# Expert outputs added from 128 stacked rows, and the overfull path as one loop on the chip

## The chip, the cores and the metric

The kernel runs on one NeuronCore of a Trainium2 chip. The metric is the device time of one execution in microseconds (us). One core has the engines TensorE (PE, with its weight loads shown as PEld), VectorE (DVE), ScalarE (ACT), GpSimd (POOL), and SyncE (SP), whose queue issues most DMAs.

## The reference, cut to what matters

Two transformer-like blocks run one after the other on 256 tokens of 1024 features, in fp32. What the change touches is the mixture of experts that closes each block: block 1 has 16 experts, block 2 has 32, and every token goes to two of them.

```python
# block 1
hid = silu(einsum('td,edf->tef', t, w_gate)) * einsum('td,edf->tef', t, w_up)
hid = hid * gates[:, :, None]
y = einsum('tef,efd->td', hid, w_down)     # 256 tokens, 16 experts, 1024 -> 512 -> 1024
# block 2, for each of 32 experts
hdn = silu(xt @ wg) * (xt @ wu)
acc = acc + cw[:, None] * (hdn @ wd)
```

## The kernel before, in words

**Weights.** All weights come in over the SP queue (`Stream`, L128) in pieces of 1 MiB, in a fixed order, into a pool of 21 tiles of 128x2048 fp32. An expert has six pieces: two each of gate, up and down.

**Dispatch.** An expert holds at most `cap` tokens, 64 in block 1 and 32 in block 2. The router gives each token a slot number in each of its experts. `dispatch` (L1140) gathers the tokens of four experts of block 1 (eight of block 2) into columns, with 0/1 matrices `pm` that DVE makes by comparing slots with an iota (L1125); the result is normalized on the way out of PSUM by DVE (L1147) and ACT (L1149).

**One expert** (`experts`). `gate_up` (L1215) multiplies by the gate and up weights into one PSUM bank; `hidden` copies (L1156), transposes (L1161; in block 2 L1163), and makes silu(gate) x up (L1166, L1168). `slots_T` makes `PT`, the 0/1 matrix from slots to tokens, (L1179, L1181, L1185), and each slot's gate value `gc` (L1183, L1187). `back()` then multiplies by the down weights (`down`, L1224). The result `py` stands on 128 rows: the slots with output features 0 to 511 (half q = 0) on rows 0 to 63, the same slots with features 512 to 1023 (q = 1) on rows 64 to 127.

**Adding an expert's output.** `gated` multiplies `py` by gate value and gain (L1197, DVE), rounds it to fp32r, the high part `yh` (L1198, ACT), and subtracts to have the low part `yl` (L1199, DVE), so that two fp32r products carry the fp32 value. `add` multiplies by `PT` into the accumulators `acc`: in block 1 `to_features` (L1242), 16 matmuls of 64 rows and 256 columns for an expert, namely two halves x four feature blocks x high and low; in block 2 `to_rows` (L1253), 8 matmuls of 64 rows and 512 columns. Both operands have 64 rows, one half at a time. In the program, an expert's addition stands between the two halves of the next expert's `gate_up`; the last expert goes by halves of its output (L1301).

**Overfull experts.** Ahead of `experts`, `overflow` handles what is over `cap`. A flag, true if any expert has more than `cap` tokens, is loaded into a register of every engine (L1313), and all five engines take `tc.If` (L1314). Its body loops over the experts on the chip (L1315); within, Python unrolls one copy of the code for each further 64 tokens: three copies in block 1, four in block 2. With these inputs the flag is 0 in both blocks, so the body is jumped over.

**Order.** A scheduler of the language decides where each engine's instructions stand, from their dependences and its own costs, so an edit in one function can move instructions of others.

## Time and profile before

| | before |
|---|---|
| median of 3 runs | 1361.27 us (1361.03 to 1363.59) |
| the profiled execution's own time | 1368.25 us |
| its span in the trace | 1366.7 us |
| mean granted TensorE clock | 0.934 |
| PE, DVE, ACT, POOL busy | 87%, 41%, 23%, 7% of the span |
| moved by DMA | 404.15 MB, 296 GB/s over the span |

The profile is of one execution; its span is from the first to the last instruction. "PEclk" is the TensorE clock that was granted, as a share of full speed. A wait of an engine is given with its releaser, as [3.79 <-PEq L1314]: 3.79 us idle, ended by PE's sequencer at line 1314. A `q` behind an engine's name is its sequencer, which takes branches and issues DMAs. A matmul's shape is written as weights, then output: 64\*128 64x256 has 64 rows of input, 128 columns of weights, and 256 columns that stream. An fp32 matmul of 128\*64 shows as two records.

### The profile page before, as it was taken

The numbers are of one execution on the slowest core, as the hardware profiler recorded it, in microseconds if no ns is written. First come the engines' busy times: TensorE is split into PE (matmuls) and PEld (weight loads), VectorE is DVE, ScalarE is ACT, GpSimd is POOL, SyncE is SP. The second block draws the span as 40 slices with busy tenths as digits, with TensorE's granted clock in tenths as the row PEclk, the third lists the DMA queues.
The fourth block names the chain that finished last, engine by engine and source line by source line (L and its number), as shares of the span: only waits on it lengthen the run. The fifth ranks groups of instructions, "written<-read, shape, count | busy, mean of one in ns | idle before, by whom it ended". The sixth has DMA issues, their size and how long they took to land. (4 is left out here: it accounts for less than half of the span.)

```text
span 1366.7 us, 20989 instructions
## 1 busy us (share of the span) xinstructions
PE 1194.2 (87%) x8690; PEld 731.7 (54%) x8690; DVE 556.7 (41%) x1418; ACT 314.4 (23%) x629; POOL 101.2 (7%) x111
## 2 busy tenths in 40 slices
PE   5899967899999986988999999879888887788786
PEld 2777757444444434886778888844323332233222
DVE  4487653322214127688655747442211221121112
ACT  3345331111101014552332224221101110010001
POOL 2421110000001003001510010000000000000000
PEclk7999888899999995999999999989997999999987
DMA  8777657799984952451236528759999999999995
GB/s 297 288 286 277 249 204 276 301 419 419 420 320 173 421 239 96 152 182 34 71 133 216 183 88 335 289 218 419 419 419 419 420 419 419 421 419 418 420 419 211
DMA packets 60520, 404.15 MB, mean 296 GB/s; under 512 B 7329, under 2 KB 7585, under 8 KB 14465
## 3 DMA queue, kind: packets, MB, share of 16 engines
q1 hardware_dynamic: 58464, 400.58, 73.5%
q10 hardware_dynamic: 1824, 2.00, 0.5%
q8 instruction: 72, 1.18, 0.3%
q0 software_dynamic: 128, 0.13, 0.1%
q14 instruction: 32, 0.25, 0.1%
HBM read 401.64 MB, written 1.05 MB: 295 GB/s over the span
## 5 line engine op out<-in xcount | busy, mean ns | idle before, releaser
L1215 PE MATMUL a<-u,u 128*32 128x512 f32 (+1 forms) x1536 | 311.4, 619 | 14.5 <-DMA u<-in_expert_w_up 7.5
L1197 DVE SCALAR_TENSOR_TENSOR gs<-a,gc,gt 128x512 f32<-128x512 f32 (+1 forms) x50 | 37.5, 750 | 304.6 <-PE a L1224 293.1
L1224 PE MATMUL a<-u,hid 128*32 128x512 f32 (+1 forms) x736 | 127.8, 619 | 37.6 <-DMA u<-in_expert_w_down 37.6
L1215 PEld LDWEIGHTS a<-u,u 128*32 128x32 f32 (+1 forms) x1536 | 71.2, 120 | 150.3 <-issue 119.7
L684 PE MATMUL a<-u,u 128*128 128x256 f32 x656 | 144.2, 298 | 2.2 <-DVE u L629 2.2
L684 PE MATMUL a<-u,hi 128*128 128x256 f32 x640 | 137.4, 306 | 0.4 <-ACT u L1529 0.4
L684 PEld LDWEIGHTS a<-u,u 128*128 128x128 f32 x656 | 107.3, 199 | 12.7 <-issue 9.2
L1156 ACT COPY gs<-a 128x512 f32<-128x512 f32 x48 | 28.1, 585 | 355.3 <-PE a L1215 353.1
L684 PEld LDWEIGHTS a<-u,hi 128*128 128x128 f32 x640 | 100.0, 193 | 15.6 <-issue 8.9
L1224 PEld LDWEIGHTS a<-u,hid 128*32 128x32 f32 (+1 forms) x736 | 31.1, 118 | 116.0 <-issue 47.8
L1198 ACT CAST u<-gs 128x512 fp32r<-128x512 f32 (+1 forms) x50 | 30.9, 618 | 186.1 <-DVE gs L1197 186.1
L1253 PE MATMUL acc<-u,PT 64*128 64x512 f32 x256 | 60.8, 468 | 13.0 <-ACT u L1198 11.2
L629 DVE TENSOR_TENSOR u<-u,hi 128x1024 fp32r<-128x1024 f32 x48 | 61.6, 1291 | 15.2 <-ACT hi L628 14.7
L628 ACT CAST hi<-u 128x1024 fp32r<-128x1024 f32 x48 | 49.8, 1047 | 68.9 <-PE a L684 60.6
L1185 DVE CAST PT<-a 128x256 fp32r<-128x256 f32 x48 | 20.4, 424 | 108.3 <-PE acc L1253 63.0
L1253 PEld LDWEIGHTS acc<-u,PT 64*128 64x128 f32 x256 | 31.8, 206 | 53.4 <-DVE u L1199 16.6
L1179 DVE TENSOR_SCALAR gp<-iota,rslot 128x128 f32<-128x128 f32 x96 | 23.0, 283 | 86.8 <-PE a L1183 78.1
L908 PE MATMUL a<-u,u 128*128 128x256 f32 x256 | 50.3, 318 | 9.2 <-DVE u L629 8.0
L629 POOL TENSOR_TENSOR u<-u,u 128x512 fp32r<-128x512 f32 (+1 forms) x22 | 44.0, 2018 | 129.8 <-ACT u L628 129.8
L1163 PEld LDWEIGHTS a<-sel,gs 128*128 128x128 f32 x256 | 35.1, 212 | 28.6 <-issue 27.1
L908 PEld LDWEIGHTS a<-u,u 128*128 128x128 f32 x256 | 41.5, 222 | 10.3 <-DVE u L629 8.2
L1181 PEld LDWEIGHTS a<-ident,gp 128*128 128x128 f32 x96 | 11.4, 141 | 65.0 <-issue 31.5
(447 smaller groups left out, 1691.2 us busy)
## 6 DMA issues: line engine op xcount, KB each, us to landing
u<-in_expert_w_gate SPq DMA_DIRECT2D x96, 1024.0 KB, 19.9
u<-in_expert_w_up SPq DMA_DIRECT2D x96, 1024.0 KB, 19.9
u<-in_expert_w_down SPq DMA_DIRECT2D x96, 1024.0 KB, 19.9
u<-in_ada_w SPq DMA_DIRECT2D x32, 1024.0 KB, 7.0
u<-in_w_in SPq DMA_DIRECT2D x19, 1024.0 KB, 4.9
u<-in_ada_w SPq DMA_DIRECT2D x32, 512.0 KB, 4.3
u<-in_attn_w_in SPq DMA_DIRECT2D x12, 512.0 KB, 8.9
u<-in_attn_w_in SPq DMA_DIRECT2D x6, 1024.0 KB, 7.0
```

Source lines behind the costliest of these rows:

```text
L628: nc.scalar.copy(h[:, o], w[:, o])
L629: (nc.vector if e == "v" else nc.gpsimd).tensor_tensor(l[:, o], w[:, o], h[:, o].bitcast(F32), ALU.subtract)
L684: c.nc.tensor.matmul(ps, a[:, k, c0:c0 + n], b[:, k], start=k == 0 and i == 0, stop=k == kn - 1 and i == 2)
L908: self.c.nc.tensor.matmul(ps[:, j * S:(j + 1) * S], a[:, k, j * P:(j + 1) * P], b[:, k], start=k + j + i == 0, stop=k == KD - 1 and i == 2 ...
L1156: nc.scalar.copy(gs, pg)
L1163: nc.tensor.matmul(pt[:, f * w:(f + 1) * w], gs[:, f * P:(f + 1) * P], fl(c.sel), start=True, stop=True)
L1179: nc.vector.tensor_scalar(gp[:, t], it, slot[:, t], None, ALU.is_equal)
L1197: nc.vector.scalar_tensor_tensor(out=y[o], in0=py[o], scalar=gc[o], in1=gt[o], op0=ALU.mult, op1=ALU.mult)
L1198: nc.scalar.copy(yh[o], y[o])
L1215: c.nc.tensor.matmul(pg[r:r + cap], xe[:, k0 + k, x0:x0 + cap], w[:, k, :], start=k0 + k < nk, stop=k0 + k >= KD - nk)
L1224: c.nc.tensor.matmul(py[r:r + cap], hT[:, f], w[:, f - f0, q * 512:(q + 1) * 512], start=f < nk, stop=f >= 4 - nk)
L1253: c.nc.tensor.matmul(acc[:, 2 * t + q], PT[H2[q], t * P:(t + 1) * P], y[H2[q], :], start=False, stop=stop and i == 1, skip_group_check=True)
```

## The change

Three things change.

1. **Stacked rows.** The high part of half q stays on that half's 64 rows and goes to column block q of a tile, and the low part is written to the other 64 rows of the same column block. One matmul of 128 rows then adds high and low together, against `PT`, which holds the same slots in both halves of its rows. `to_features` issues 8 matmuls instead of 16 for an expert, `to_rows` 4 instead of 8. `gated` casts and subtracts twice 64x512 in place of once 128x512, and the subtraction reads rows of one half and writes rows of the other.
2. **A loop on the chip.** The body of `overflow` stands once, in a second loop on the chip that lowers the slot by 64 each time, in place of three or four unrolled copies.
3. **Which side comes first.** `tc.If` gets `preferred_fallthrough_block=False`: behind the compare comes the false, empty side, an unconditional branch over the body.

Counted in the two built programs, PE's jump over the body goes from 677 to 262 instructions in block 1 and from 827 to 254 in block 2; DVE's first jump before is over 86. PE has 17577 instructions in all, 19069 before.

```diff
@@ -1188,23 +1188,26 @@
     return PT, gc
 
 
-def gated(c, ep, py, gc, gt, o=slice(0, P)):
-
-    nc = c.nc
-    yh, yl = c.ys[0]
+def gated(c, ep, py, gc, gt, qs=(0, 1)):
+
+
+    yy = c.ys[0]
     c.ys.reverse()
     y = ep.tile([P, 512], F32, name="gs", bufs=2)
-    nc.vector.scalar_tensor_tensor(out=y[o], in0=py[o], scalar=gc[o], in1=gt[o], op0=ALU.mult, op1=ALU.mult)
-    nc.scalar.copy(yh[o], y[o])
-    nc.vector.tensor_tensor(yl[o], y[o], yh[o].bitcast(F32), ALU.subtract)
-    return yh, yl
+    o = slice(0, P) if len(qs) == 2 else H2[qs[0]]
+    c.nc.vector.scalar_tensor_tensor(out=y[o], in0=py[o], scalar=gc[o], in1=gt[o], op0=ALU.mult, op1=ALU.mult)
+    for q in qs:
+        c.nc.scalar.copy(yy[H2[q], q], y[H2[q]])
+    for q in qs:
+        c.nc.vector.tensor_tensor(yy[H2[1 - q], q], y[H2[q]], yy[H2[q], q].bitcast(F32), ALU.subtract)
+    return yy
 
 
 def split_rows(c):
 
     c.uys = c.un.raw()
-    y = c.uys.bitcast(F32R).rearrange("p (i a d) -> p i a d", i=2, a=2)
-    c.ys = [(y[:, i, 0], y[:, i, 1]) for i in range(2)]
+    y = c.uys.bitcast(F32R).rearrange("p (i q d) -> p i q d", i=2, q=2)
+    c.ys = [y[:, i] for i in range(2)]
 
 
 def gate_up(c, pg, xe, x0, cap, w, a, k0, kn):
@@ -1234,24 +1237,22 @@
 
 def to_features(c, acc):
 
-    def add(ys, PT, stop=False, qs=(0, 1)):
+    def add(yy, PT, stop=False, qs=(0, 1)):
         for q in qs:
             for b in range(4):
                 fb = 4 * q + b
-                for i, y in enumerate(ys):
-                    c.nc.tensor.matmul(acc[:, fb // 2, (fb % 2) * S:(fb % 2 + 1) * S], y[H2[q], b * P:(b + 1) * P],
-                                       PT[H2[q], :], start=False, stop=stop and i == 1, skip_group_check=True)
+                c.nc.tensor.matmul(acc[:, fb // 2, (fb % 2) * S:(fb % 2 + 1) * S], yy[:, q, b * P:(b + 1) * P], PT,
+                                   start=False, stop=stop, skip_group_check=True)
     return add
 
 
 def to_rows(c, acc):
 
-    def add(ys, PT, stop=False, qs=(0, 1)):
+    def add(yy, PT, stop=False, qs=(0, 1)):
         for q in qs:
             for t in range(2):
-                for i, y in enumerate(ys):
-                    c.nc.tensor.matmul(acc[:, 2 * t + q], PT[H2[q], t * P:(t + 1) * P], y[H2[q], :],
-                                       start=False, stop=stop and i == 1, skip_group_check=True)
+                c.nc.tensor.matmul(acc[:, 2 * t + q], PT[:, t * P:(t + 1) * P], yy[:, q],
+                                   start=False, stop=stop, skip_group_check=True)
     return add
 
 
@@ -1299,7 +1300,7 @@
         for f in range(4):
             o = (q * nk + f % nk) * cap
             nc.tensor.matmul(py[o:o + cap], hT[:, f], w[:, f], start=f < nk, stop=f >= 4 - nk)
-        add(gated(c, ep, py, gc, gt, H2[q]), PT, True, (q,))
+        add(gated(c, ep, py, gc, gt, (q,)), PT, True, (q,))
         end(q)
 
 
@@ -1311,13 +1312,14 @@
     wg, wu, wd = (c.I[f"expert_w_{a}{x}"][:NE * 2 * P * 2048].rearrange("(e h p n) -> e h p n", h=2, p=P, n=2048)
                   for a in ("gate", "up", "down"))
     rv = nc.values_load(flag[0:1, 0:1], min_val=0, max_val=1)
-    with tc.If(rv > 0):
+    with tc.If(rv > 0, preferred_fallthrough_block=False):
         with tc.For_i(0, NE, 1) as e:
-            for base in range(cap, S, 64):
-                so = ep.tile([P, 2, 1], F32, name="oso")
-                go = ep.tile([P, 2, 1], F32, name="ogo")
-                nc.vector.tensor_scalar(so, slot[:, :, bass.ds(e, 1)], -float(base), None, ALU.add)
-                nc.vector.tensor_copy(go, gate[:, :, bass.ds(e, 1)])
+            so = ep.tile([P, 2, 1], F32, name="oso")
+            go = ep.tile([P, 2, 1], F32, name="ogo")
+            nc.vector.tensor_scalar(so, slot[:, :, bass.ds(e, 1)], 64.0 - cap, None, ALU.add)
+            nc.vector.tensor_copy(go, gate[:, :, bass.ds(e, 1)])
+            with tc.For_i(0, -(-(S - cap) // 64), 1):
+                nc.vector.tensor_scalar(so, so, -64.0, None, ALU.add)
                 xo = ep.tile([P, KD, 64], F32, name="oxe")
                 dispatch(c, ep, tok, so, 0, 1, 64, xo)
                 PT, gc = slots_T(c, ep, so, go, 64)
```

In what follows, lines of the changed kernel are two or three further on: gate_up is L1218, down L1227, the addition of block 1 L1244, the flag's load L1314 and the branch L1315.

**Where the order moves.** PE's queue around the first overflow path, before, from the last dispatch matmuls to the loop's head (`acc<-u,ident` puts the residual into the accumulator):

```order
L1140 MATMUL a<-pm,u_662 128x256 x16
L1450 MATMUL acc<-u_67,ident 128x512 x4
L1313 TENSOR_LOAD rfl_2207
L1314 COMPARE_AND_BRANCH
L1315 COMPARE_AND_BRANCH
L1315 UNCONDITIONAL_BRANCH x2
L2408 BRANCH_PREFETCH_HINT
```

and now:

```order
L1140 MATMUL a<-pm,u_662 128x256 x16
L1452 MATMUL acc<-u_67,ident 128x512 x4
L1314 TENSOR_LOAD rfl_2207
L1315 COMPARE_AND_BRANCH
L1315 UNCONDITIONAL_BRANCH
L1316 COMPARE_AND_BRANCH
L1316 UNCONDITIONAL_BRANCH x2
L2410 BRANCH_PREFETCH_HINT
```

Behind the compare (L1315) there is now an unconditional branch, and then the two nested loops' heads (L1316 and, further on, L1321); before, the outer loop's head followed the compare.

PE's queue in block 1's experts, an addition near the end of the down matmuls, before:

```order
L1224 MATMUL a<-u_2615,hid 64x512 x4
L1224 MATMUL a<-u_2137,hid 64x512 x4
L1161 MATMUL a<-ident,gs 128x128 x4
L1215 MATMUL a<-u_2138,u_2143 64x512
L1242 MATMUL acc<-PT,u_2213 128x256 x16
L1215 MATMUL a<-u_2139,u_2143 64x512
```

and now:

```order
L1227 MATMUL a<-u_2374,hid 64x512 x4
L1227 MATMUL a<-u_2137,hid 64x512 x4
L1161 MATMUL a<-ident,gs 128x128 x4
L1181 MATMUL a<-ident,gp 128x128 x2
L1218 MATMUL a<-u_2138,u_2143 64x512
L1244 MATMUL acc<-PT,u_2213 128x256 x4
L1183 MATMUL a<-rgate_2195,gp 128x1 x2
L1244 MATMUL acc<-PT,u_2213 128x256 x4
L1218 MATMUL a<-u_2139,u_2143 64x512
```

The addition is 4 + 4 matmuls in place of 16, and the next expert's slot matrices (L1181, L1183) have come ahead of it and between its halves; before, they stood further on, between the halves of gate_up.

PE's queue in block 1's experts, the last dispatch of four experts (L1140), before its first part:

```order
L1215 MATMUL a<-u_2214,u_2143 64x512
L1140 MATMUL a<-pm,u_661 128x256 x4
L1140 MATMUL a<-pm,u_662 128x256
L1215 MATMUL a<-u_2215,u_2143 64x512
L1140 MATMUL a<-pm,u_662 128x256 x3
L1215 MATMUL a<-u_2615,u_2143 64x512
L1215 MATMUL a<-u_2215,u_2143 64x512
```

and now all of it:

```order
L1227 MATMUL a<-u_2137,hid 64x512 x4
L1227 MATMUL a<-u_2138,hid 64x512 x4
L1161 MATMUL a<-ident,gs 128x128 x4
L1140 MATMUL a<-pm,u_661 128x256 x12
L1140 MATMUL a<-pm,u_662 128x256 x6
L1140 MATMUL a<-pm,u_661 128x256 x4
L1140 MATMUL a<-pm,u_662 128x256 x10
L1218 MATMUL a<-u_2139,u_2143 64x512
```

Before, eight of the 32 matmuls stood 5 + 3 in the middle of a gate_up and the other 24 after the next L1161; now all 32 stand in one run behind L1161.

## Rows read from the trace of the kernel before

**Rows 1.** Windows by stage: us, busy of PE PEld DVE ACT POOL, PEclk, DMA, GB/s.
```profile
256.00:262.00 6.00, 5.95 (x20) 2.29 (x22) 1.99 (x8) 0.00 (x0) 0.00 (x0) 0.72 1.02 422
300.00:400.00 100.00, 98.62 (x534) 46.38 (x532) 21.68 (x58) 13.65 (x27) 0.00 (x0) 1.00 1.01 414
...
963.00:1345.00 382.00, 313.33 (x1881) 119.75 (x1871) 71.72 (x185) 41.66 (x88) 0.00 (x0) 0.95 1.01 419
1314.80:1328.50 13.70, 12.47 (x42) 4.47 (x43) 2.22 (x5) 0.89 (x2) 0.00 (x0) 0.50 1.01 420
```

**Rows 2.** The timeline of PE, 275 to 505: first row after each end of fourteen periods.
```profile
277.88 0.44 PE L1181 MATMUL a<-ident,gp 128*128 128x128 f32 x2
...
500.23 0.66 PE L1161 MATMUL a<-ident,gs 128*128 128x128 f32 x4
```

**Rows 3.** The branch on the flag (L1314), by engine: ns min/median/max, first and last start.
```profile
L1314 PEldq COMPARE_BRANCH  x2: 3359/5289/7219, 248.4 to 900.7; - x2
L1314 DVEq COMPARE_BRANCH  x2: 56/64/72, 249.8 to 901.8; - x2
```

**Rows 4.** The timeline around the first branch: start, us, instruction, [idle before <- releaser].
```profile
248.67 3.59 PE L1450 MATMUL acc<-u,ident 128*128 128x512 f32 x8
...
256.05 6.21 PE L1215 MATMUL a<-u,u 128*64 128x512 f32 x20 [3.79 <-PEq L1314]
```

**Rows 5.** The timeline around the second branch.
```profile
899.97 1.22 PE L1140 MATMUL a<-pm,u 128*128 128x256 f32 x8 [0.81 <-DVE rcm L1097]
...
901.81 0.56 ACT L1149 ACTIVATE u<-a,mod,A2b 128x256 f32<-128x256 f32 x1 [1.46 <-DVE u L1147]
...
904.45 5.34 PE L1215 MATMUL a<-u,u 128*32 128x512 f32 x32 [3.26 <-PEq L1314]
```

**Rows 6.** The timeline of PE, one dispatch and one addition between two halves of gate_up.
```profile
305.97 4.05 PE L1140 MATMUL a<-pm,u 128*128 128x256 f32 x32
...
313.54 1.79 PE L1242 MATMUL acc<-PT,u 64*128 64x256 f32 x16
315.26 3.65 PE L1215 MATMUL a<-u,u 128*64 128x512 f32 x16
```

**Rows 7.** The timeline of an addition that follows close on its down matmuls.
```profile
402.38 0.75 DVE L1197 SCALAR_TENSOR_TENSOR gs<-a,gc,gt 128x512 f32<-128x512 f32 x1 [6.55 <-PE a L1224]
...
403.17 0.62 ACT L1198 CAST u<-gs 128x512 fp32r<-128x512 f32 x1 [3.61 <-DVE gs L1197]
...
403.82 0.69 DVE L1199 TENSOR_TENSOR u<-gs,u 128x512 fp32r<-128x512 f32 x1 [0.68 <-ACT u L1198]
403.85 0.38 PE L1242 MATMUL acc<-PT,u 64*128 64x256 f32 x1
...
404.56 1.66 PE L1242 MATMUL acc<-PT,u 64*128 64x256 f32 x15 [0.33 <-DVE u L1199]
```

**Rows 8.** The timeline of PE, a dispatch split around a pair of gate_up.
```profile
358.66 0.86 PE L1140 MATMUL a<-pm,u 128*128 128x256 f32 x5
359.44 1.07 PE L1215 MATMUL a<-u,u 128*64 128x512 f32 x2
...
361.00 3.65 PE L1215 MATMUL a<-u,u 128*64 128x512 f32 x14
```

**Rows 9.** The timeline of PE, the fifth period, and of the last expert's second half.
```profile
349.08 0.30 PE L1181 MATMUL a<-ident,gp 128*128 128x128 f32 x1 [0.67 <-DVE gc L1187]
...
511.71 2.37 PE L1242 MATMUL acc<-PT,u 64*128 64x256 f32 x15 [1.86 <-DVE u L1199]
```

**Rows 10.** The timeline of the tail.
```profile
1356.88 1.41 DVE L1199 TENSOR_TENSOR u<-gs,u 64x512 fp32r<-64x512 f32 x2
1356.93 0.61 ACT L1198 CAST u<-gs 64x512 fp32r<-64x512 f32 x1 [0.23 <-DVE gs L1197]
...
1357.62 0.96 PE L1253 MATMUL acc<-u,PT 64*128 64x512 f32 x3 [0.36 <-DVE u L1199]
...
1359.98 2.07 PE L1253 MATMUL acc<-u,PT 64*128 64x512 f32 x4 [1.40 <-ACT u L2228]
```

## The prediction

> **What bounds the kernel now.** I read the windows by stage first, then the branch line of the overflow path, then the engine timelines around it, around an addition in each block, and at the end. Block 1's experts (some 256 to 505 us) are bound by PE: 98.6 us busy of 100 at clock 1.00 [rows 1]. The fourteen expert periods from 277.88 to 500.23 take 222.35 us [rows 2]. Block 2's experts are bound by the weight DMA: 419 GB/s at a DMA share of 1.01 over 382 us, with PE busy 313.3 of them at clock 0.95 [rows 1]. PE work that is saved there is worth nothing; an earlier start of the DMA stream and a shorter tail are. Between the stages, up to the second branch, both kernels have the same order on PE, so time gained in block 1 is carried through.
>
> The sum is made against the profiled execution, whose own time is 1368.25 us (span 1366.7); the median of the runs is 1361.27, 7 us below it. The sum of differences is applied to both.
>
> **The branch around the overflow path, block 1.** The flag is 0, so no engine runs the body. DVE's compare-and-branch took 56 to 72 ns, PE's took 7219 and 3359 ns [rows 3]; counted in the built programs, DVE jumps over 86 instructions there, PE over 677 in block 1 and 827 in block 2. DVE is at its branch at 249.8 [rows 3]; PE's last matmuls before its own start at 248.67 and end by 252.26, and yet its next one comes at 256.05, after 3.79 us in which it waited for its own sequencer [rows 4]. So what is late is PE's jump. After, the body stands once instead of three and four times and the additions in it are halved: PE jumps over 262 and 254 instructions, and the flag's false side comes right behind the compare. No row shows a jump of 262. It lies between DVE's (0.06 us) and PE's (3.4 us). I take DVE's and leave 0.4 us of meeting of the engines: **-3.4 us**. [...]
>
> After the idle time the granted clock is 0.72 over 256 to 262 [rows 1]: twenty matmuls of gate_up take 6.21 us [rows 4], where sixteen at full clock take 3.65, so twenty 4.56 [rows 6]. Without the gap the clock has no reason to fall, since PE was at 1.00 before it: **-1.65 us**.
>
> **Each addition in block 1.** Sixteen 64-row matmuls take 1.72 us from start to start (313.54 to 315.26), 0.108 each. 128-row matmuls of the same 256 columns take 4.05 us for 32 [rows 6], some 0.125 each. Eight stacked ones are at least 8 x 0.108 = 0.86, at most 1.72. I take 8 x 0.125 plus 0.14 for the change of tile shape = 1.14, by the nearest row: -0.58 each, over fourteen periods **-8.1 us**.
>
> [...]
>
> What pays for it: ACT casts twice 64x512 (0.61 us each) in place of 128x512 once (0.62 [rows 7]), DVE subtracts twice 64x512 (1.41 us for two [rows 10]) in place of once (0.69 [rows 7]). Both have room (DVE 21.7, ACT 13.7 us busy of 100 [rows 1]). The subtraction now writes to the other 64 partitions. No row shows such an operation; between 0.70 (the same shape, straight) and 1.4 (twice it), I take 0.70, the nearest shape. In the first five periods half a gate_up, 3.5 us, lies between the end of down and the addition, which covers the chain of 3.0 us (multiply 0.75, two casts, two subtractions).
>
> **The order in block 1.** Fewer matmuls make the scheduler place things otherwise.
> - Two dispatches of four experts (L1140) are split before: eight of 32 matmuls stand 5 + 3 around one pair of gate_up, 2.34 us from 358.66 to 361.00 [rows 8]. That pair alone takes 1.00 instead of 0.44, the eight need 1.00 in one run, and the fourteen that follow lose another 0.5. In the new order all 32 stand together: 2.34 - 1.00 - 0.44 + 0.5 = 1.4 each, **-2.8**.
> - The fifth period holds two selections (L1181, L1183) back to back, with 0.67 us of idle time between them [rows 9], the down matmuls split around them; after, they stand apart: **-1.0**.
> - In six periods the addition follows close on the down matmuls: one pair of gate_up, then the first matmul at 403.85 and the other fifteen at 404.56, because DVE's subtraction is not done [rows 7]: 0.71 - 0.11 = 0.60 lost. After, the order is L1161, L1181, a pair of gate_up, four matmuls, L1183, four matmuls. PE gets to the first four some 0.6 + 0.3 + 1.0 = 1.9 us after the down's end [rows 2, 8]; the first low half is ready at 0.1 + 0.75 + 0.04 + 0.61 + 0.03 + 0.69 + 0.05 = 2.3 [rows 7, 10], so 0.4 is lost; the second is covered by L1183 and the first four. 0.17 each, **-1.0**.
>
> Together the fourteen periods go from 222.35 to 209.4. If crossing partitions costs 1.4 us, each of some seven close periods loses 0.7: +5, which stays in the range.
>
> **The end of block 1.** The addition ahead of the last expert's down matmuls is one of the close ones: -0.3. The last expert's own two halves wait 1.86 us for DVE and take 2.37 for fifteen matmuls [rows 9]; seven of these fall away, 7 x 0.11 = 0.8, and -0.2 for a wait that is shorter because no matmul of the second half stands behind the first half's: **-1.3 us**.
>
> **The branch, block 2.** PE's last matmuls start at 899.97 for 1.22 us and the next at 904.45 after 3.26 us of waiting for its sequencer. ACT's last normalization runs from 901.81 to 902.37 [rows 5]. So with a short jump all engines meet at 902.4 to 902.6. The SP queue issues the next weights behind the same meeting, and from there the DMA runs without a break to the end [rows 1]: **-1.9 us** for everything behind.
>
> **The tail.** After the last weights every addition stands on the path: three matmuls 0.96 at 1357.62, four 2.07 at 1359.98 [rows 10]. Halving the last gives -0.9, the one before -0.25, and the previous expert's addition (sixteen cut to half, less the second cast and subtraction now in its way) -0.25: **-1.4 us**.
>
> Sum: -3.4 - 1.65 - 8.1 - 2.8 - 1.0 - 1.0 - 1.3 - 1.9 - 1.4 = **-22.6 us**: 1345.7 for a profiled execution like the one shown, **1338.7** for the median.
>
> **Rivals.**
> - *Only the matmuls count.* The transfers take the gain from the order: weights of block 1 still come in during its last experts, and PE nears them by what it gains. Then -4.8 is lost: 1343.5. For it: the DMA ran near its full rate behind 256 too [rows 1], so its lead is finite. Against: the list of waits shows no DMA wait before PE in that stage. 0.13.
> [...]
> - *64-row matmuls already run in pairs.* Then -8.1 and the tail's -1.2 fall away: 1348. [...] 0.05.
> - *Slower: the clock in block 2's experts.* PE has slack there now and gets more: four matmuls fewer for an expert, and so longer idle stretches. From 1314.8 to 1328.5 the granted clock was 0.50 in that stage, while the DMA went on at 420 GB/s [rows 1]; before, the lag was recovered in the next expert. An expert's six pieces of 1 MiB take 15.0 us at 419 GB/s; PE is busy 313.3 / 382 of that, 12.3 us, mostly at full clock. At half clock that is between 12.3 and 24.6; in the middle, some 19. It decides from the point where the half level outlasts one expert: each further one costs 4 us; six in all take back the gain, ten give 1338.7 + 40 = 1379. For it: clock 0.95 over the stage, so it happens now. Against: no stretch cost anything so far. 0.06.
>
> **How the numbers follow.** Forecast 0.60, rivals 0.13, 0.10, 0.05, 0.06; the rest, 0.06, are mixtures of these with a smaller gain. About 0.2% (2.7 us) is what a measurement of this kernel can tell from no change. Faster: 0.60 + 0.13 + 0.10 + 0.05 + 0.01 = 0.89; same 0.04; slower 0.07. The range reaches down to 1332 (stacked additions at 0.86 us each give -3.9, close periods without their 0.4 another -2.8) and up to 1350 (the second, third and fourth cases and the +5 of crossing); what is left out is the slower case and the mixtures.
>
> **What would show it.** The PE branch line of the changed profile under 0.3 us, twice, and no stretch below full clock behind the first. The addition's group in block 1 with 128 rows, half the instructions, near 0.125 us each from start to start. Fourteen periods of 209 us. The subtraction of 64x512 at 0.70. The first weight issue of block 2 at ACT's last normalization. It would be wrong if PE's branch is still over 3 us, if a DMA wait appears before PE between 400 and 490, or if block 2's experts show clock 0.5 over more than two in a row.

## The result and the profile after

The changed kernel takes **1344.39 us** (median of 4 runs, 1341.36 to 1345.95) against 1362.43 of the kernel before (4 runs, 1361.03 to 1369.01): a ratio of **0.9867, interval 0.9845 to 0.9888**, 18.0 us less. The prediction was 1338.7 (1332 to 1350), a gain of 22.6 us.

| | before | after |
|---|---|---|
| span of the profiled execution | 1366.7 us | 1339.8 us |
| mean granted TensorE clock | 0.934 | 0.941 |
| PE, DVE, ACT busy | 1194.2, 556.7, 314.4 us | 1146.8, 592.5, 347.0 us |

The two profiled executions differ by 26.9 us, more than the medians, so they are compared stage by stage and not by their spans.

The branch on the flag in the changed kernel, now L1315 (ns min/median/max); it answers to [rows 3]:

```profile
L1315 PEldq COMPARE_BRANCH  x4: 64/234/397, 246.5 to 882.1; - x4
L1315 DVEq COMPARE_BRANCH  x4: 47/50/60, 248.5 to 882.8; - x4
```

There are four entries for two branches: the compare, which falls through, and behind it the jump over the body. On PE the compares took 98 and 64 ns and the jumps 397 and 371 ns, where one compare took 7219 and 3359 before, in block 1 and block 2.

The timeline around the first and around the second branch, as [rows 4] and [rows 5]:

```profile
247.37 3.60 PE L1452 MATMUL acc<-u,ident 128*128 128x512 f32 x8
...
251.83 7.09 PE L1218 MATMUL a<-u,u 128*64 128x512 f32 x32 [0.86 <-PEq L1315]
```

```profile
880.73 1.21 PE L1140 MATMUL a<-pm,u 128*128 128x256 f32 x8 [0.80 <-DVE rcm L1097]
...
882.07 0.33 SPq L128 DMA_DIRECT2D u<-in_expert_w_gate  x1
882.57 0.56 ACT L1149 ACTIVATE u<-a,mod,A2b 128x256 f32<-128x256 f32 x1 [1.45 <-DVE u L1147]
...
883.23 3.64 PE L1218 MATMUL a<-u,u 128*32 128x512 f32 x32 [1.28 <-ACTq L1315]
```

PE's wait ahead of gate_up falls from 3.79 to 0.86 us, and all 32 of its records take 7.09 us at a granted clock of 1.00 (251.83 to 258.95 us). In block 2 PE starts 0.10 us after ACT's last normalization (882.57 + 0.56), and SP asks for the next weights even before that.

PE's timeline in block 1's experts: the start of the first period, an addition far from its down matmuls and the matmuls behind it, a dispatch, a close period from its first row to gate_up, the eleventh period, the start of the last expert, and its last addition. They answer to [rows 2, 6 to 9]:

```profile
271.97 0.44 PE L1181 MATMUL a<-ident,gp 128*128 128x128 f32 x2
...
276.75 1.21 PE L1244 MATMUL acc<-PT,u 128*128 128x256 f32 x8
277.89 3.65 PE L1218 MATMUL a<-u,u 128*64 128x512 f32 x16
...
298.88 4.42 PE L1140 MATMUL a<-pm,u 128*128 128x256 f32 x32
...
375.41 0.66 PE L1161 MATMUL a<-ident,gs 128*128 128x128 f32 x4
375.90 0.38 PE L1181 MATMUL a<-ident,gp 128*128 128x128 f32 x2
376.21 1.07 PE L1218 MATMUL a<-u,u 128*64 128x512 f32 x2
377.69 0.74 PE L1244 MATMUL acc<-PT,u 128*128 128x256 f32 x4 [0.40 <-DVE u L1202]
378.26 0.50 PE L1183 MATMUL a<-rgate,gp 128*128 128x1 f32 x4
378.63 0.72 PE L1244 MATMUL acc<-PT,u 128*128 128x256 f32 x4
379.28 6.65 PE L1218 MATMUL a<-u,u 128*64 128x512 f32 x29
...
418.76 0.72 PE L1140 MATMUL a<-pm,u 128*128 128x256 f32 x4
422.71 1.92 PE L1140 MATMUL a<-pm,u 128*128 128x256 f32 x14 [3.23 <-DVE gs L1198]
425.33 1.93 PE L1140 MATMUL a<-pm,u 128*128 128x256 f32 x14 [0.69 <-DVE hid L1168]
...
483.57 0.66 PE L1161 MATMUL a<-ident,gs 128*128 128x128 f32 x4
...
494.95 1.65 PE L1244 MATMUL acc<-PT,u 128*128 128x256 f32 x8 [2.29 <-DVE u L1202]
```

An addition between two halves of gate_up takes 1.14 us (276.75 to 277.89), not 1.72. The close period starts with transposes and slot matrices, has one pair of gate_up, waits 0.40 us for DVE, and has its addition in two parts. The fourteen periods go from 271.97 to 483.57: 211.6 us. In the eleventh, PE waits 3.23 and 0.69 us for DVE. DVE's timeline there:

```profile
411.59 0.58 DVE L292 COPY u<-ident 128x256 f32<-128x256 f32 x2 [3.09 <-PE a L1218]
...
421.77 0.22 DVE L313 TENSOR_TENSOR u<-u 128x64 int32<-128x64 int32 x1
421.92 0.74 DVE L1198 SCALAR_TENSOR_TENSOR gs<-a,gc,gt 128x512 f32<-128x512 f32 x1
```

From 411.59 to 421.77 DVE works through small operations that build masks for block 2; only then does it multiply (L1198) the down result that the dispatch's banks wait for. In the kernel before the same wait took 1.94 us; PE's timeline of its eleventh period:

```profile
438.22 1.35 PE L1140 MATMUL a<-pm,u 128*128 128x256 f32 x9 [1.94 <-DVE gs L1197]
```

The tail, PE's timeline, as [rows 10]:

```profile
1332.31 0.73 PE L1254 MATMUL acc<-u,PT 128*128 128x512 f32 x2 [1.98 <-DVE u L1202]
1334.44 0.73 PE L1254 MATMUL acc<-u,PT 128*128 128x512 f32 x2 [1.40 <-ACT u L2230]
```

Two matmuls of 0.73 us where there were three and four of 0.96 and 2.07.

**Where the time went, by stage.** Five stretches, each worked out from PE's timeline of the profiled execution: from the accumulators' first matmul to the first gate_up (1), from there to the first of the fourteen periods (2), the fourteen periods (3), from there to the first matmul of block 2 (L530) (4), and from the last record of block 2's dispatch to its first gate_up (5). The last columns compare each kernel's median with that of the kernel before on the same chip.

| kernel | 1 | 2 | 3 | 4 | 5 | median us (before) | ratio (interval) |
|---|---|---|---|---|---|---|---|
| before | 7.38 | 21.83 | 222.3 | 15.4 | 3.54 | 1362.4 | |
| after | 4.45 | 20.14 | 211.6 | 14.6 | 1.56 | 1344.4 (1362.4) | 0.9867 (0.9845 to 0.9888) |
| e1 stacked only | 6.06 | 21.84 | 222.6 | 14.9 | 3.91 | 1359.2 (1360.3) | 0.9990 (0.9973 to 1.0008) |
| e2 path only | 4.46 | 20.14 | 218.3 | 15.3 | 1.56 | 1351.9 (1360.3) | 0.9944 (0.9923 to 0.9964) |
| e3 empty first only | 9.99 | 22.57 | 222.3 | 15.3 | 4.90 | 1367.8 (1360.3) | 1.0047 (1.0021 to 1.0073) |
| e4 loop only | 4.05 | 20.14 | 218.5 | 15.1 | 1.64 | 1350.2 (1360.7) | 0.9924 (0.9901 to 0.9948) |
| e5 64 rows in turn | 6.52 | 21.00 | 214.9 | 14.0 | 3.80 | 1348.7 (1360.3) | 0.9909 (0.9890 to 0.9929) |
| e6 path, 64 rows in turn | 4.36 | 20.14 | 207.2 | 13.6 | 1.56 | 1340.3 (1361.5) | 0.9845 (0.9825 to 0.9865) |
| e7 after, additions pinned | 4.46 | 20.14 | 210.8 | 14.9 | 1.56 | 1344.1 (1361.5) | 0.9865 (0.9844 to 0.9886) |
| e8 before, banks two on | 7.38 | 21.83 | 218.5 | 18.0 | 3.98 | 1360.6 (1360.7) | 0.9988 (0.9974 to 1.0003) |
| e9 after, masks later | 4.50 | 20.14 | 208.1 | 14.5 | 1.56 | 1343.4 (1361.5) | 0.9875 (0.9855 to 0.9895) |
| e10 e6, pinned, masks later | 4.46 | 20.14 | 204.0 | 13.9 | 1.56 | 1334.3 (1361.5) | 0.9809 (0.9788 to 0.9830) |
| e11 e6, program order, masks later | 4.36 | 21.84 | 194.2 | 13.5 | 1.56 | 1329.2 (1360.7) | 0.9761 (0.9741 to 0.9781) |
| e12 e11 with stacked rows | 4.45 | 20.15 | 195.8 | 15.0 | 1.56 | 1326.5 (1360.7) | 0.9739 (0.9722 to 0.9757) |

For after against before the five stretches give -2.93, -1.69, -10.7, -0.8 and -1.98, together -18.1 us: the whole difference of the medians, 18.0, but for the tail. The spans of the two profiled executions differ by 8.8 us more. Of these, 5.7 lie between block 2's first gate_up and the end, 4.4 of them behind the last down matmuls, where the profiled execution of the kernel before ran slowly; 1.8 lie in block 2 up to its dispatch and 1.3 ahead of stretch 1, where nothing was changed.

**A caution for stretch 3.** In the eleventh period PE waits for DVE, and behind that wait the granted clock falls to 0.50 in some profiles and not in others: over the whole period it is 1.00 in the kernel before (435.1 to 457.2 us) and in the changed kernel (418.35 to 440.63). In e1 it is 0.50 from 430.0 to 435.3 us, and half a gate_up takes 5.30 us from start to start (433.35 to 438.65) instead of 3.58:

```profile
433.35 5.37 PE L1218 MATMUL a<-u,u 128*64 128x512 f32 x16
```

In e6 it is 0.50 from 417.2 to 419.0 us, and 28 matmuls of the dispatch take 4.92 us (417.17 to 422.09), where 32 take 3.99 in its third period:

```profile
417.17 4.99 PE L1140 MATMUL a<-pm,u 128*128 128x256 f32 x28 [3.21 <-DVE gs L1197]
```

Worked out from the starts of the matmuls behind the wait, this costs an estimated 2.5 us in e1, 2.9 in e5, and 1.4 to 1.6 in e2, e4, e6, e7 and e8, but nothing in the kernel before, e3 and the changed kernel. The length of the waits doesn't separate them: 1.94 and 0.36 us before and 3.23 and 0.69 in the changed kernel, without a fall, and 1.94 and 0.38 in e5, with one. Each kernel has one profile, so sums of stretch 3 that differ by less than some 3 us are compared by their single periods.

### The profile page after: what moved, and what is told of

Its sections match the earlier page's. It is cut to its first block, busy times and chain, and to the rows that moved or that the text cites. A ratio compares the mean times of both kernels' runs of the same rounds, so it can differ in the third digit from the quotient of the medians.

```text
span 1339.8 us, 20574 instructions
## 1 busy us (share of the span) xinstructions
PE 1146.8 (86%) x8434; PEld 705.4 (53%) x8434; DVE 592.5 (44%) x1464; ACT 347.0 (26%) x675; POOL 101.7 (8%) x111
## 5 line engine op out<-in xcount | busy, mean ns | idle before, releaser
L1218 PE MATMUL a<-u,u 128*32 128x512 f32 (+1 forms) x1536 | 297.8, 614 | 36.2 <-DMA u<-in_expert_w_up 25.3
L1198 DVE SCALAR_TENSOR_TENSOR gs<-a,gc,gt 128x512 f32<-128x512 f32 (+1 forms) x50 | 37.5, 750 | 367.5 <-PE a L1227 360.2
L1227 PE MATMUL a<-u,hid 128*32 128x512 f32 (+1 forms) x736 | 135.5, 623 | 40.7 <-DMA u<-in_expert_w_down 40.7
L1218 PEld LDWEIGHTS a<-u,u 128*32 128x32 f32 (+1 forms) x1536 | 71.1, 119 | 176.6 <-issue 106.9
L684 PE MATMUL a<-u,u 128*128 128x256 f32 x656 | 141.5, 292 | 1.9 <-DVE u L629 1.9
L684 PEld LDWEIGHTS a<-u,u 128*128 128x128 f32 x656 | 104.4, 193 | 12.7 <-issue 9.2
L1200 ACT CAST u<-gs 64x512 fp32r<-64x512 f32 x96 | 59.2, 616 | 183.3 <-DVE gs L1198 182.2
L1227 PEld LDWEIGHTS a<-u,hid 128*32 128x32 f32 (+1 forms) x736 | 33.3, 119 | 124.2 <-DMA u<-in_expert_w_down 52.1
L1202 DVE TENSOR_TENSOR u<-gs,u 64x512 fp32r<-64x512 f32 x96 | 65.9, 686 | 27.2 <-ACT u L1200 25.3
L908 PE MATMUL a<-u,u 128*128 128x256 f32 x256 | 49.0, 312 | 9.2 <-DVE u L629 8.0
L1254 PE MATMUL acc<-u,PT 128*128 128x512 f32 x128 | 44.4, 460 | 5.2 <-DVE u L1202 3.6
L1140 PE MATMUL a<-pm,u 128*128 128x256 f32 x256 | 40.8, 315 | 8.1 <-DVE gs L1198 3.2
L908 PEld LDWEIGHTS a<-u,u 128*128 128x128 f32 x256 | 40.4, 216 | 10.3 <-DVE u L629 8.2
L1254 PEld LDWEIGHTS acc<-u,PT 128*128 128x128 f32 x128 | 22.3, 208 | 44.1 <-DVE u L1202 34.3
L763 PE MATMUL e<-u,u 128*128 128x256 f32 x288 | 40.1, 306 | 5.5 <-ACT u L591 5.0
```

The costliest lines, as they stand in the source:

```text
L684: c.nc.tensor.matmul(ps, a[:, k, c0:c0 + n], b[:, k], start=k == 0 and i == 0, stop=k == kn - 1 and i == 2)
L763: T.matmul(p[:, j * S:(j + 1) * S], l, r, start=(h, j, k, n) == (0, 0, 0, 0), stop=(h, k, n) == (1, 3, 2), skip_group_check=True)
L908: self.c.nc.tensor.matmul(ps[:, j * S:(j + 1) * S], a[:, k, j * P:(j + 1) * P], b[:, k], start=k + j + i == 0, stop=k == KD - 1 and i == 2 ...
L1140: nc.tensor.matmul(ps[:, jj * m:(jj + 1) * m], h[:, t, k * P:(k + 1) * P], pm[:, t], start=i + jj + t == 0, stop=i + t == 2, skip_group_ch ...
L1198: c.nc.vector.scalar_tensor_tensor(out=y[o], in0=py[o], scalar=gc[o], in1=gt[o], op0=ALU.mult, op1=ALU.mult)
L1200: c.nc.scalar.copy(yy[H2[q], q], y[H2[q]])
```

## The experiments

**e1: the stacked rows alone.** The kernel before with the new `gated`, `split_rows`, `to_features` and `to_rows`; the overflow path stays unrolled.

```diff
 def overflow(...):
-    with tc.If(rv > 0, preferred_fallthrough_block=False):
+    with tc.If(rv > 0):
...
-            with tc.For_i(0, -(-(S - cap) // 64), 1):
+            for base in range(cap, S, 64):
```

(the changed kernel, with `overflow` taken back whole)

> Only the stacked rows (gated, split_rows, to_features, to_rows), the overflow path as before with its unrolled copies. Theory (the parts are separate): PE's branch at the flag still takes over 3 us and the clock below full speed follows it, while an addition of eight 128-row matmuls between two halves of gate_up takes 1.14 us instead of 1.72; the fourteen periods of block 1's experts then take some 211 to 215 us instead of 222.4, and the time is 9 to 12 us under the kernel before. Rival (the gain is mostly the branch and the order that the short body brings): fourteen periods above 217 us and less than 6 us gained.

Measured: ratio 0.9990, no change that can be told. Additions far from their down matmuls take what the theory said (periods 12.95 instead of 13.53 us), yet the fourteen periods sum to 222.6, as the rival said (above 217). A close period got longer, 15.47 to 15.49 us instead of 15.19 to 15.21. PE's timeline of one in e1:

```profile
392.86 1.07 PE L1218 MATMUL a<-u,u 128*64 128x512 f32 x2
394.56 1.47 PE L1244 MATMUL acc<-PT,u 128*128 128x256 f32 x8 [0.63 <-DVE u L1202]
396.61 0.44 PE L1181 MATMUL a<-ident,gp 128*128 128x128 f32 x2 [0.58 <-DVE gc L1187]
...
397.31 6.65 PE L1218 MATMUL a<-u,u 128*64 128x512 f32 x29
```

The eight matmuls wait 0.63 us for the first subtraction and then take 1.47 us instead of 1.14, since the second comes later (argued from the order of the subtractions), and the next slot matrices (L1181) wait 0.58 us for a bank that DVE empties late, behind its two subtractions. PE has half the matmuls and stands still for as long. The sum holds something else too: the tenth and eleventh periods together grew by 2.4 us, about what the lower clock is estimated to cost there, and the other twelve fell by 2.1. So at an even clock e1 would gain an estimated 2 us in this stage, a quarter of the 8.1 that was reckoned for it. **In e1, half the matmuls of an addition was worth 0.58 us where the addition is PE-bound, and nothing where it waits for DVE.** With the changed path in place the same stacking gives more: from e2 to the changed kernel, which differ in nothing else, the fourteen periods fall from 218.3 to 211.6.

**e2: the path alone.** The kernel before with the changed `overflow` and nothing else.

```diff
-    with tc.If(rv > 0):
+    with tc.If(rv > 0, preferred_fallthrough_block=False):
...
-            for base in range(cap, S, 64):
+            with tc.For_i(0, -(-(S - cap) // 64), 1):
```

> Only the overflow path (one loop on the chip, empty side first), the additions of 64 rows as before. Theory: PE's branch takes under 0.5 us in both blocks, PE's first gate_up of block 1 waits 0.9 us instead of 3.8 and runs at full clock (2.9 + 1.7 us), block 2's first weights are asked for 2 us earlier; the fourteen periods stay near 222 us unless the order moves; 6 to 8 us under the kernel before. [...]

Measured: ratio 0.9944, 8.5 us. The branch is as predicted (stretches 1, 2 and 5: -2.92, -1.69, -1.98), and the fourteen periods fell by 4.1 us on top, though no instruction of theirs was changed. e8 asks why.

**e3: the empty side first alone.**

```diff
-    with tc.If(rv > 0):
+    with tc.If(rv > 0, preferred_fallthrough_block=False):
```

> Only the empty side first; the body stays unrolled (677 and 827 instructions on PE). [...] Rival (what decides is that the false side comes right behind the compare): all branch rows under 0.5 us and 6 to 7 us gained.

Measured: ratio 1.0047, **slower** by 7.5 us, where the rival had 6 to 7 us gained and all branch rows under 0.5 us; the long jump stays long. The branch line and PE's timeline of e3:

```profile
L1314 PEldq COMPARE_BRANCH  x4: 81/2126/5931, 244.3 to 900.7; - x4
```

```profile
244.53 3.60 PE L1450 MATMUL acc<-u,ident 128*128 128x512 f32 x8
254.51 1.97 PE L1215 MATMUL a<-u,u 128*64 128x512 f32 x4 [6.39 <-issue]
```

The compares are short now (81 ns at the least); the jumps behind them take up to 5931 ns. Before, the jump was the compare itself, and PE took it at 248.4 with its last matmuls still running until 252.26, so 3.8 of its 7.2 us were covered [rows 3, 4]. With the empty side first the engines meet before the jump: PE's last matmuls of e3 end at 248.13, and then the whole jump lies bare, until 254.51. In stretch 1 this is 2.6 us more than before, in stretch 5 1.4, and 0.7 in stretch 2, behind the longer gap: 4.7 us of the 7.5, and within the interval of the difference (2.9 to 9.9 us).

**e4: the loop alone.** e2 without the empty side first.

```diff
-    with tc.If(rv > 0, preferred_fallthrough_block=False):
+    with tc.If(rv > 0):
```

> Of the overflow path only the loop on the chip; the empty side is not put first. Theory (the length of the jump decides, and the empty side first only moves the jump behind the meeting of the engines): PE's branch takes under 0.5 us in both blocks, the time is within 2 us of the run with the whole path changed (1351.9 against 1360.3 of the kernel before), the fourteen periods 218.3 as there. Rival (the short jump needs the empty side first): PE's branch over 3 us and at most 5 us gained, all of it in the periods.

Measured: ratio 0.9924, 10.5 us; its interval overlaps that of e2. The branch line:

```profile
L1314 PEldq COMPARE_BRANCH  x2: 416/430/445, 242.8 to 886.0; - x2
```

The time is 1.7 us from e2's and the periods are as there, both as the theory said. PE's jump, here over 278 and 262 instructions counted in the built program, takes 0.45 and 0.42 us, whichever side is first. So **in these fourteen kernels the length of the jump decides**. In the nine kernels whose body stands once, the jump takes 0.28 to 0.45 us. In the five with the unrolled body (677 and 827 instructions in the kernel before) it takes 5.9 to 7.2 us in block 1 and 3.4 to 4.2 in block 2; for e3 the 4.2 is the fourth entry, 4155, of which the median shows only the mean with a compare of 98. How the time grows between 278 and 677 instructions, and what in a long jump takes the time, none shows. DMA moved 389 GB/s while the kernel before jumped in block 1 (248.40 to 255.62 us) and 10 GB/s in block 2 (900.70 to 904.06). That the transfers of weights make the jump longer in block 1 is argued from these two places, not tried.

The empty side first, the third part of the change, is not what pays: without it stretch 1 is 4.05 us instead of 4.46 in e2, since the short jump too is then taken while matmuls run (it starts at 242.8, PE's last matmuls end at 247.30), and stretch 5 is 1.64 instead of 1.56.

**e5: 64-row matmuls in turn.** The kernel before, with the loops of the addition turned round, so that matmuls on rows 0 to 63 and 64 to 127 alternate.

```diff
-        for q in qs:
-            for b in range(4):
-                for i, y in enumerate(ys):
+        for i, y in enumerate(ys):
+            for b in range(4):
+                for q in qs:
```

> The kernel before with one thing changed: the 64-row matmuls of an addition are issued alternately for the two halves of the rows (first half, second half, first half, ...), 16 and 8 as before. Theory (64-row matmuls run one after the other, as 0.108 us each showed): an addition in block 1 still takes 1.7 us and the time stays within 2 us of the kernel before. Rival (two 64-row matmuls on different rows run at once when they are issued in turn): an addition takes 0.9 to 1.1 us, fourteen periods some 213 us, and 8 to 10 us are gained without any stacking.

Measured: ratio 0.9909, 11.6 us gained by the order of loops alone. The rival was right, with an addition a little over its 0.9 to 1.1 us. An addition of e5, PE's timeline:

```profile
275.75 1.22 PE L1242 MATMUL acc<-PT,u 64*128 64x256 f32 x16
276.90 3.65 PE L1215 MATMUL a<-u,u 128*64 128x512 f32 x16
```

Sixteen matmuls of 64 rows take 1.15 us from start to start (275.75 to 276.90) instead of 1.72 [rows 6], as eight stacked ones do (1.14). In the trace they start two by two, the first two at 275.746 and 275.749 and the next at 275.967 and 275.973. So here two 64-row matmuls on different rows, issued in turn, run at once; in the kernel before, where the eight of one half go ahead of the eight of the other, one took 0.108 us [rows 6]. Close periods take 14.26 us, against 15.2: with one cast and one subtraction of 128x512, the whole addition is ready at once.

**e6: the path and 64 rows in turn.** e5's loops with the changed `overflow`; nothing is stacked.

> The changed overflow path, and the 64-row matmuls of an addition issued in turn for the two halves of the rows, with one cast and one subtraction of 128x512 as in the kernel before; nothing stacked. Theory (an addition's cost on PE is the same whether two 64-row matmuls run at once or one of 128 rows does, and stacking only adds a cast and a subtraction): periods with the addition between two halves of gate_up 12.95 us, close ones some 14.0 (0.3 under the changed kernel's 14.31, because the chain is shorter), fourteen periods 208 to 212, time within 3 us of the changed kernel, rather below it. Rival (stacking is better in all periods): fourteen periods above 214 and 3 us or more over the changed kernel.

Measured: ratio 0.9845, 21.3 us under the kernel before; the changed kernel's ratio is 0.9867, and the intervals overlap, so the two are not told apart. The fourteen periods take 207.2 us, a little under the theory's range. The close ones take 13.95 against 14.31 in the changed kernel, whose addition waits 0.40 us for DVE while this one waits for nothing: the second cast and subtraction that stacking needs cost 0.36 us there.

**e7: additions pinned.** The changed kernel, each matmul of block 1's additions held in program order on PE.

```diff
-                c.nc.tensor.matmul(acc[...], yy[:, q, b * P:(b + 1) * P], PT, ...)
+                c.tc.keep_in_program_order(c.nc.tensor.matmul(acc[...], yy[:, q, b * P:(b + 1) * P], PT, ...))
```

> The changed kernel with block 1's addition matmuls held in program order on PE, so that each addition stays between the two halves of the next gate_up. Theory (the close periods of 14.31 us are the order's doing: the addition waits for DVE, and one pair of gate_up stands alone twice): they fall to some 13.4 us, nine of them save 8 us, the fourteen periods take 203 to 206 us, and the time falls 6 to 9 us under the changed kernel. Rival (the weights' DMA sets those periods): a DMA wait stands before gate_up or down, and less than 3 us are gained.

Measured: ratio 0.9865, as the changed kernel; neither the theory's 6 to 9 us nor the rival's DMA wait. The close periods are 14.07 to 14.09 us, only 0.23 less. PE's timeline of one:

```profile
377.34 0.66 PE L1161 MATMUL a<-ident,gs 128*128 128x128 f32 x4
377.83 0.38 PE L1181 MATMUL a<-ident,gp 128*128 128x128 f32 x2
378.14 1.07 PE L1218 MATMUL a<-u,u 128*64 128x512 f32 x2
379.14 0.61 PE L1183 MATMUL a<-rgate,gp 128*128 128x1 f32 x4
379.68 3.65 PE L1218 MATMUL a<-u,u 128*64 128x512 f32 x14
383.25 1.22 PE L1245 MATMUL acc<-PT,u 128*128 128x256 f32 x8
```

The addition now stands behind half a gate_up and waits for nothing; but a pair of gate_up, which is the two records of one fp32 matmul, still stands alone between L1181 and L1183. That pair takes 1.00 us (378.14 to 379.14) and the fourteen records behind it 3.57, where all sixteen in one piece take 3.58 (273.17 to 276.75 in the changed kernel): **1.0 us a period for a pair that stands alone**, as in the kernel before [rows 8]. The starts in the trace show why. In a run, the records of two matmuls, one for each half of the 128 output rows, start together (379.677 and 379.684). The lone matmul's two records start one after the other (378.139 and 378.619) with nothing beside them, and of the seven matmuls behind it the last is again without a partner (382.303 and 382.732). In the sum it was counted as unchanged, and it was; but it is the larger part of what makes a close period long. No DMA wait of PE appeared in the fourteen periods.

**e8: why the order moved.** The kernel before, with one statement behind the overflow path.

```diff
         overflow(c, ep, flag, "", 16, 64,
                  (th, tl), slot, gate, add, gt)
+        c.turn += 2
```

> The kernel before with one statement added behind the overflow path: the counter that hands out PSUM banks in turn is raised by two, which is how the shorter body shifts it (five banks for one copy of the body, fifteen for three; four banks in turn). Theory (the order of block 1's experts moved because of this counter, not because anything in the experts is shorter): the fourteen periods take 218.3 us as in the run with the path alone changed, PE's branch still takes over 3 us, and the time is 3 to 5 us under the kernel before. Rival (the order moved because the scheduler reckons with the body's length): fourteen periods of 222.3 us as before.

Measured: fourteen periods of 218.45 us, and the single periods of e2 within 0.2 us (14.38, 14.88, 18.57, 14.87 and so on). So the theory holds for the periods: **the shorter body takes five PSUM banks from the rotation instead of fifteen, and this shift alone, with no shorter body, makes the scheduler place the experts' work otherwise**, with e2's period times. The time was another matter: ratio 0.9988, at most 0.26% (3.5 us) gained, where the theory said 3 to 5 us. In the profiled execution 2.7 us are lost again in stretch 4, where the last expert's matmuls run slowly, at a granted clock of 0.69 over 496 to 504 us (they take 5.42 us in the kernel before and in e2):

```profile
496.18 7.73 PE L1301 MATMUL a<-u,hid 128*64 128x512 f32 x16
```

Whether this happens in each of its runs can't be told from one profile; why e8's time moved by less than its periods is left open.

**e9: masks later.** The changed kernel, DVE's mask building held behind the work traced before it.

```diff
             st.size(len(st.slots) - 3)
-            masks2(c)
+            last = next(i for i in reversed(nc.cur_bb.bb.instructions) if i.engine == nc.vector.engine)
+            with tc.issue_after(last):
+                masks2(c)
```

> The changed kernel with DVE's mask building for block 2 (lines 258 to 330) held behind the work of the expert before it, instead of ahead of the eleventh period. Theory (the eleventh period's 22.28 us hold 3.2 + 0.7 us of waiting for DVE, which is working through the masks): it falls to some 18.8 us, like the seventh, and 2 to 4 us are gained, less what the masks delay two experts later. Rival (the wait only moves to where the masks are built then): the sum of the fourteen periods stays within 1 us of 211.6.

Measured: the eleventh period falls from 22.28 to 18.77 us, the fourteen to 208.1 and no other period grew. PE's timeline of it:

```profile
415.51 0.66 PE L1161 MATMUL a<-ident,gs 128*128 128x128 f32 x4
415.92 2.43 PE L1140 MATMUL a<-pm,u 128*128 128x256 f32 x18
418.97 1.93 PE L1140 MATMUL a<-pm,u 128*128 128x256 f32 x14 [0.62 <-DVE hid L1168]
```

The wait for L1198 is gone, the one for L1168 stays. The time did not follow: ratio 0.9875 against the changed kernel's 0.9867, where 3.5 us would be 0.26%; the two were measured on different chips with intervals of 0.2% to either side, so this is neither shown nor excluded. In the profile, the stretch from block 2's start to its branch, where nothing was changed, is 5 us longer than in the changed kernel's profile (388.8 against 383.5 us from L530 to the last dispatch record); other kernels show 384.8 to 388.9 there. So the theory is shown for the period alone.

**e10: 64 rows in turn, pinned, masks later.** e6, e7's pin on its 64-row matmuls, and e9's later masks.

```diff
-                    c.nc.tensor.matmul(acc[...], y[H2[q], b * P:(b + 1) * P], PT[H2[q], :], ...)
+                    c.tc.keep_in_program_order(c.nc.tensor.matmul(acc[...], y[H2[q], b * P:(b + 1) * P], PT[H2[q], :], ...))
```

> Changed overflow path, 64-row matmuls in turn, block 1's additions held in program order, masks later. Theory (all four are separate): fourteen periods some 195 to 202 us and a time of 1330 to 1337, under both kernels. Rival (with PE faster the weights of block 1's last experts are late): DMA waits before gate_up or down in the last periods, and a time no better than the changed kernel less 4 us.

Measured: ratio 0.9809, 27.2 us under the kernel before. Fourteen periods 204.0, a little over the theory's 195 to 202, since the lone pair stays (14.07 to 14.09); the time, 1334.3 us, is within its 1330 to 1337. No DMA wait appeared. The four are not separate: against e6 the eleventh period falls from 22.18 to 18.00 us, while the pin makes the close ones 0.13 longer.

**e11: all of PE's work in block 1's experts in program order.** e6 with `keep_in_program_order` on every matmul of gate_up, down, `hidden`, `slots_T` and the additions in block 1's experts, and masks later.

```diff
+def pin(c, ins):
+    if c.pinned:
+        c.tc.keep_in_program_order(ins)
...
-        c.nc.tensor.matmul(pg[r:r + cap], xe[:, k0 + k, x0:x0 + cap], w[:, k, :], ...)
+        pin(c, c.nc.tensor.matmul(pg[r:r + cap], xe[:, k0 + k, x0:x0 + cap], w[:, k, :], ...))
```

> Changed overflow path, 64-row matmuls in turn for the two halves (nothing stacked), all of PE's work in block 1's experts held in program order, masks later. Theory: every period without a dispatch takes 12.95 us, one with a dispatch 16.8, the fourteen 192 to 194, and the time is 1321 to 1327. Rival (the weights of block 1's last experts are then late): DMA waits before gate_up or down in the last periods, and a time above 1329.

Measured: ratio 0.9761, 1329.2 us, over the theory's 1321 to 1327 and at the rival's bound of 1329. Ten periods are 12.94 to 12.96 us, three with a dispatch 16.8; only the last is longer (14.48). One DMA wait, of 0.20 us before gate_up, appears there, so in the last period the weights are what ends last; e12 waits 0.69 us at the same place. Stretch 2 is 1.7 us longer than in e12; PE's timeline shows where:

```profile
258.65 0.66 PE L1166 MATMUL a<-ident,gs 128*128 128x128 f32 x4 [1.31 <-ACT gs L1161]
259.23 8.78 PE L1220 MATMUL a<-u,u 128*64 128x512 f32 x32
```

Thirty-two records take 8.78 us behind a pause of 1.31 us; in e12 the same pause stands there and they take 7.09. The granted clock over 256 to 262 us is 0.83 here and 1.00 in e12.

**e12: the same, with stacked rows.** e11 with `gated`, `split_rows`, `to_features` and `to_rows` of the change.

```diff
-                    pin(c, c.nc.tensor.matmul(acc[...], y[H2[q], b * P:(b + 1) * P], PT[H2[q], :], ...))
+                pin(c, c.nc.tensor.matmul(acc[...], yy[:, q, b * P:(b + 1) * P], PT, ...))
```

> The same with the stacked rows of the change in place of the 64-row matmuls in turn. Theory (one 128-row matmul costs PE what two 64-row matmuls at once do, and the second cast and subtraction are covered where the addition stands half a gate_up later): the fourteen periods within 1.5 us of the run with 64 rows in turn and the times within 2 us of each other. Rival (the second cast and subtraction still cost): 3 us or more slower than that run.

Measured: ratio **0.9739** (0.9722 to 0.9757), 1326.5 us, the fastest of all, 34.2 us under the kernel before; its interval overlaps e11's. Fourteen periods 195.8 against 194.2 in e11, a difference as the theory gave (1.5); the medians lie 2.7 us apart, the theory said 2. A period of e12, PE's timeline:

```profile
368.55 0.44 PE L1186 MATMUL a<-ident,gp 128*128 128x128 f32 x2
368.82 0.50 PE L1188 MATMUL a<-rgate,gp 128*128 128x1 f32 x4
369.19 0.64 PE L1166 MATMUL a<-ident,gs 128*128 128x128 f32 x4
369.75 3.65 PE L1223 MATMUL a<-u,u 128*64 128x512 f32 x16
373.33 1.21 PE L1249 MATMUL acc<-PT,u 128*128 128x256 f32 x8
```

Slot matrices, transposes, half a gate_up, the addition: nothing waits. A period with a dispatch and no wait takes 17.13 us with stacked rows and 16.8 with 64 rows in turn (third period: 17.12 in after and e9, 16.77 in e5 and e6). That DVE and ACT, which empty the dispatch's banks, are busier with stacked rows is the likely reason, but was not tried. The whole gap of 1.5 us is three such periods and the 0.5 us that the last one waits longer for weights. In stretch 4 the stacked kernel is 1.4 us longer, and in stretch 2 1.7 us shorter by the clock; which of the two kernels is faster is not settled.

## Why the prediction was right and where it was not

- **The jump, block 1** (-3.4): -2.93. A short jump is cheap, as said (0.42 and 0.45 us in e4). Its price in the changed kernel was taken as DVE's 0.06 us, though no row of before shows a jump of 262 instructions; it is 0.37 to 0.40 us, an amount between the bounds, and so the sign "under 0.3 us, twice" was missed. The empty side first, which the prediction counted with the gain, costs some 0.4 us here (e2 against e4).
- **The clock behind it** (-1.65): -1.69, as predicted.
- **An addition** (-0.58): 1.72 to 1.14 us where it is far from its down matmuls, as predicted; that the 0.14 us in it are for a change of tile shape was the author's estimate, and no run shows them apart. The term that was mis-sized is "over fourteen periods -8.1 us". In the close periods an addition is not PE-bound: in e1 the far ones gain 0.58 and the close ones lose 0.28, and an estimated 2 us are left at an even clock. From e2 to the changed kernel stacking gives 6.6 us. In the changed kernel the close ones are 0.9 us shorter than before (15.2 to 14.31): 0.33 by the new order (15.2 to 14.87 in e2), and 0.56 by the halved matmuls once DVE's chain no longer bars them.
- **The order** (-4.8 in three parts): it did move the sum, by 4.1 us alone (e2). Its sizes were read from the built program's order and did not rest on the cause. The cause that was named, "fewer matmuls", is not what moved it: e8 shows the rotation of PSUM banks, which the number of copies in the overflow body shifts, and e1, which has fewer matmuls, keeps the split dispatches and has no slot matrices ahead of the addition.

The two terms above together, period by period, after against before:

| periods | reckoned | measured | what differs |
|---|---|---|---|
| first four | -2.3 | -2.0 | the dispatch takes 4.35 us instead of 3.99 |
| fifth | -1.6 | -0.95 | |
| sixth and seventh | -2.7 | -2.8 | one dispatch is split no more |
| eighth, ninth, twelfth, thirteenth | -0.75 each | -0.88 each | |
| fourteenth | -0.75 | 0 | |
| tenth and eleventh | -2.7 | -1.4 | longer waits for DVE |
| all | -12.9 | -10.7 | |

In the eleventh, a wait for DVE of 1.94 us became 3.23, and one of 0.36 became 0.69. That the same masks stand ahead of the multiplication in DVE's queue was in the trace; that they would cost more was not thought of. The first growth is the order's: e2 and e6, with one subtraction as before, wait 3.20 and 3.21 us. The tenth period, no longer holding part of the dispatch, is 3.4 us shorter, so PE reaches the dispatch sooner behind the start of the masks (425.04 for a period that starts at 435.15 before, 411.59 for one at 418.35 now). The second growth goes with the second subtraction: e2 waits 0.31 us there. That PE ran behind these waits at full clock in the profile of the changed kernel, and not in e2's, is luck of some 1.4 us in this sum.

- **The end of block 1** (-1.3): -0.8. The last addition is shorter (1.65 us for eight matmuls instead of 2.37 for fifteen), but its wait for DVE grew from 1.86 [rows 9] to 2.29 us instead of getting shorter.
- **The branch, block 2** (-1.9): -1.98, as predicted.
- **The tail** (-1.4): some -0.5. It had been sized by an execution whose tail ran slowly: 20.3 us from the start of the last down record (L1224; L1227 in the changed kernel) to the end of the span. By the same measure, kernels with 64 rows one after the other (e2, e3, e4, e8) take 16.5 to 17.3 us, those with stacked rows (after, e1, e7, e9, e12) 15.9 to 16.8; the -0.5 is the difference of their means, and the two ranges overlap.
- **The crossing of partitions**: 0.686 us mean for 32 subtractions of 64x512, the price of the straight one (1.41 us for two [rows 10]), as taken.
- **Rivals.** *Only the matmuls count* fell: PE's matmuls wait for no DMA in the fourteen periods. The second of the four cases, at 0.10, a jump as late as before, fell: PE's jumps take 0.40 and 0.37 us. *64-row matmuls in pairs* does not hold for the order of issue in the kernel before (0.108 us for one [rows 6]), but e5 shows that this order was a choice: in turn, they give what stacking gives (1.15 against 1.14 us), with less work for ACT and DVE. *Slower by the clock in block 2* did not come: PE's clock there is 0.95 as before over 963 to 1320.

The sum missed by 4.6 us of 22.6: 2.2 in the periods, 0.9 in the tail, 0.5 at each of the first jump and the end of block 1; the rest is the spread of the medians.

## What to carry to other kernels

Halved matmuls paid only in the places where PE is what ends last; where an addition waits for the vector engine's preparation, the second cast and subtraction ate the gain (e1: fourteen periods of 222.6 us against 222.3), so move the addition away first, here by holding the order. Issue small-row matmuls in turn for different rows before you rebuild their operands: here it cost nothing and gave the same (1.15 us for an addition against 1.14). Keep skipped code short on the engine that has most instructions (here PE's jump took 0.28 to 0.45 us over a body that stands once, 3.4 to 7.2 us over the unrolled one), and check an edit that should not touch a stage for what it shifts there, such as a rotation of banks.

## What was not expected

- Putting the empty side first made the **long** jump dearer (7.5 us by the medians, e3), since the meeting of the engines then came before the jump and none of it was hidden behind running matmuls (PE idle for 6.39 us in block 1, 3.79 before).
- One matmul of gate_up that stands alone costs 1.0 us more: it takes 1.00 us and the seven behind it 3.57, where all eight in one run take 3.58. With PE's order held and the masks later, the stage falls from 211.6 to 195.8 us (e12), more than the change itself gained there.
- Behind the same pause of 1.31 us the granted clock over 256 to 262 us is 1.00 in e12 and 0.83 in e11, and behind the waits of the eleventh period it is 1.00 in some kernels and 0.50 in others; a stage with waits can't be priced to within some 3 us from one profile.
- A counter of banks, raised by two, moves fourteen periods by 3.9 us (e8).
